# Two FFN layers: the first product by seven products of halves, and each FFN in two parts

## The chip, the cores and the metric

The kernel runs on one core of a Trainium2 chip, in one launch. The metric is the device time of one execution in microseconds (us). Five engines work side by side, each through its own list of instructions: PE multiplies matrices (PEld loads their stationary operand), DVE, ACT and POOL work on elements, SP issues the transfers from main memory. An instruction waits until what it reads is written and the buffer that it writes is free; what stands behind it on that engine waits with it.

## What is computed

The reference is a decoder trunk of two layers on x of 512 tokens by 1024 channels. Each layer has a mixer and a gated feed-forward network (FFN), and a layer norm behind each. The change is in the FFN alone:

```
def swiglu(x, w_in, w_out):
    h = x @ w_in                       # 1024 x 5632: gate columns, then up columns
    return (jax.nn.silu(h[..., :D_FF]) * h[..., D_FF:]) @ w_out
...
        x = layer_norm(ALPHA * x + mix, ln_mix_g[layer], ln_mix_b[layer])
        x = layer_norm(ALPHA * x + swiglu(x, ffn_w_in[layer], ffn_w_out[layer]),
                       ln_ffn_g[layer], ln_ffn_b[layer])
```

D_FF is 2816, and all is float32.

## The kernel before

Every float32 product is made of three products of rounded parts: `split` (L82 to L85) writes a rounded copy hi of its source (ACT, L84) and the rest lo = source − hi (DVE, or POOL for some, L85), and `mm3` (L87 to L90) issues the matmuls hi·hi, hi·lo and lo·hi into one PSUM bank. The transposed x stands in `xh` and `xl`: 1024 channels in 8 blocks of 128 (`KD`), 512 tokens beside each other. The plain x is kept in `xs` (the tiles x0 to x3 of 128 tokens, which the residual uses).

`ffn(l)` (L293) runs for each layer l. **First product:** for each of the 22 blocks n of 128 hidden columns, `load_cols` (L103) brings the gate block and the up block (512 KB each, into the pool `raw` of 3 buffers) and splits them into `wt` (8 buffers); `project` (L148) issues 2 × 8 × 3 = 48 matmuls of 512 tokens for the two; then ACT makes silu of the gate (L316), DVE multiplies by the up half (L318), and the result h is split into the tiles `hh` and `hl` that the second product reads. At block n = 6 (`XN`) `late_affine` (L192 to L202) is called: the norm ahead left x in `xs` without its scale and bias, and 16 element-wise operations of 128x512 on DVE put them in, in time for the residual; two transfers bring the vectors. **Second product:** `out_proj` (L286) takes 11 pairs kp of row blocks of w_out. A first pass makes output columns 0 to 511 for all four token tiles in four banks (two `fl`, two `sc`), a second pass columns 512 to 1023 (banks `py`, `cv`, `fl`, and at the very end `fl` and `sc`); of that pass 5 pairs are kept resident so that token tiles end one after the other. `residual` (L174 to L177) adds a finished bank to ALPHA times x, and `norm` (L204) follows.

PSUM has two banks `fl`, two `sc`, and one each of `py` and `cv` for all this, and two for transposes. A scheduler puts every engine's instructions in order when the program is built: it follows the order in which the code issues them, moves instructions ahead where it finds an engine idle in its own model, and honours the offset that `late_affine` gives its operations (a lower priority). On PE that holds in both FFNs; a fixed order for PE (`manual_schedule`) is used in the odd mixer alone. A buffer of a pool is handed on when the last reader of what it held is done: this makes the first instruction that writes the new tile wait for that reader.

Of the kernel before, what the change touches and what calls it, by code (L numbers as in the profile page):

```python
# [40 lines left out]
FIRST = 2  # L41
DFIRST = 2
DG = 1
XA = 2
XN = 6
# [13 lines left out]
def trunk(ctx, tc, x, ev_w_in, ev_conv_w, ev_pool_w, ev_pool_scale, ev_w_out, od_w_in,  # L59
# [109 lines left out]
    def load_gb(gb, g, b):  # L169
        nc.sync.dma_start(gb[:, 0, :], g.partition_broadcast(P))  # L170
        nc.sync.dma_start(gb[:, 1, :], b.partition_broadcast(P))
        return gb

    def residual(t, cols, acc, st):  # L174
        xc = xs[t][:, cols]
        nc.vector.scalar_tensor_tensor(xc, xc, ALPHA, acc, op0=ALU.mult, op1=ALU.add)
        nc.vector.bn_stats(st, xc)  # L177
# [26 lines left out]
    def norm(t, st, gb, ln):  # L204
# [11 lines left out]
        for a, b in PIECES:  # L216
            xc, g, b_ = xs[t][:, a:b], gb[:, 0, a:b], gb[:, 1, a:b]
# [12 lines left out]
    class OutProj:  # L230
# [3 lines left out]
        def __init__(self, w, order, lhs, resident, resident_pool=lambda kp: None, eng=None):  # L234
            self.w, self.order, self.lhs, self.resident = w, order, lhs, resident
            self.resident_pool, self.eng = resident_pool, eng
# [27 lines left out]
        def second(self, gb, ln):  # L264
            KP, order = len(self.order), self.order
            for t in range(NT):
                residual(t, slice(0, 512), self.accs[t][0][0], self.sts[t][:, 0, :])
                self.accs[t] = None
# [4 lines left out]
            for i in range(streamed):  # L273
                ws = self.load(order[i], 512)
                for t in range(NT):
                    self.step(t, i, ws)
            ws = [self.load(kp, 512, self.resident_pool(kp)) for kp in order[streamed:]]
            for t in range(NT):
                for part in range(len(self.accs[t])):
# [3 lines left out]
                    residual(t, slice(512 + cols.start, 512 + cols.stop), acc, self.sts[t][:, 1 + part, :])  # L283
# [8 lines left out]

    def ffn(l):  # L293
        w_in, w_out = ffn_w_in[l], ffn_w_out[l]
        with tc.tile_pool(name=f"ffn{l}", bufs=1) as hp:
            pairs = []
            gb = hp.tile([P, 2, D], F32, tag="gb", name="gb") if l else None
            for n in range(NF):
                if n == XN:
                    late_affine(ln_mix_g[l], ln_mix_b[l], nc.vector)  # L300
                if n == 4 and l:
                    load_gb(gb, ln_ffn_g[l], ln_ffn_b[l])
# [17 lines left out]
            out_proj(gb, 1 + 2 * l, w_out, list(range(NF // 2)), lambda k: [y[:, k % 2, :] for y in pairs[k // 2]],  # L320
# [537 lines left out]
```

## Time and profile before

| | us |
|---|---|
| median of 3 runs | 1117.99 (1117.77 to 1118.32) |
| the profiled execution, by the clock of the runs | 1118.16 |
| its span, first to last instruction | 1116.4 |
| FFN 0 in the trace: first product / second product | 159.7 to 394 / 394 to 516 |
| FFN 1: first product / second product | 746 to 988 / 988 to 1109 |

A profile is of one execution. The page lists busy time by engine, the chain of work that ended last, and groups of like instructions by line, with the mean duration of one and the idle time ahead; other views show one engine's instructions in order of time, or sums over a stretch. A granted clock of 1.00 is PE at full speed.

### The profile page before, as it was taken

The page shows a single profiled execution, that of the slowest core. Times are in us where ns is not written, and L with a number is a line of the kernel's source. Part 1 is how long each engine was busy: PE and PEld are TensorE (multiplying, and loading weights), DVE is VectorE, ACT ScalarE, POOL GpSimd, SP SyncE. Part 2 cuts the span into 40 slices and gives each one's busy share as a digit, 9 for nine tenths or more (in the row PEclk, how much of TensorE's full clock was granted, in tenths as well). Part 3 has the DMA queues.
Part 4 walks back from the last instruction along what each step waited for, and adds up shares of the span by engine and source line. Part 5 has one row for each costly group of instructions (what it writes and reads, how often), then busy time and mean ns, then how long its engine had stood idle before and what let it go on. Part 6 is the DMA issues. An engine that isn't in the chain of part 4 may idle for free.

```text
span 1116.4 us, 13508 instructions
## 1 busy us (share of the span) xinstructions
PE 1079.8 (97%) x5371; PEld 910.6 (82%) x5371; DVE 547.4 (49%) x821; ACT 395.5 (35%) x613; POOL 176.1 (16%) x160
## 2 busy tenths in 40 slices
PE   7999999999999999999999958999999999999997
PEld 7888898888888888889878746889888888888886
DVE  4845364633333322436689978564553333332426
ACT  4333134222233221223566838634232222222210
POOL 2000300000000000012797942520000000000003
PEclk9999999999999999999999979999999999999999
DMA  6423403343333222440332221333343333332312
GB/s 202 125 88 116 144 1 114 114 116 101 102 97 94 95 95 95 135 130 2 87 104 75 88 85 58 95 95 95 95 132 95 95 95 100 104 98 95 109 42 76
DMA packets 150332, 108.30 MB, mean 97 GB/s; under 512 B 5256, under 2 KB 131768, under 8 KB 150270
## 3 DMA queue, kind: packets, MB, share of 16 engines
q1 hardware_dynamic: 149648, 107.11, 31.9%
q8 instruction: 42, 0.69, 0.2%
q10 hardware_dynamic: 622, 0.34, 0.1%
q14 instruction: 20, 0.16, 0.1%
HBM read 103.17 MB, written 2.10 MB: 94 GB/s over the span
## 4 chain that ended last, share of the span: by engine, by line
PE 85%; DVE 7%; ACT 3%; POOL 3%; issue 1%; DMA 1%; SPq 0%; POOLq 0%; ACTq 0%
PE fl L88 11%; PE fl L89 11%; PE fl L90 11%; PE sc L89 9%; PE sc L90 9%; PE sc L88 9%; PE py L88 4%; PE py L89 4%; PE py L90 4%; PE cv L89 4%; PE cv L90 4%; PE cv L88 4%; DVE cv L466 2%; POOL convs L460 1%; DVE yc L85 1%
## 5 line engine op out<-in xcount | busy, mean ns | idle before, releaser
L84 ACT ACTIVATE w<-raw 128x1024 fp32r<-128x1024 f32 x176 | 185.9, 1060 | 538.1 <-PE sc L89 180.7
L85 DVE TENSOR_TENSOR w<-raw,w 128x1024 fp32r<-128x1024 f32 x148 | 180.7, 1224 | 287.5 <-ACT w L84 287.5
L85 POOL TENSOR_TENSOR w<-raw,w 128x1024 fp32r<-128x1024 f32 x28 | 67.4, 2415 | 450.6 <-ACT w L84 427.5
L89 PE MATMUL sc<-xl,w 128*128 128x512 f32 (+1 forms) x360 | 129.9, 361 | 0.0
L90 PE MATMUL sc<-xh,w 128*128 128x512 f32 (+1 forms) x360 | 129.6, 361 | 0.0
L88 PE MATMUL sc<-xh,w 128*128 128x512 f32 (+1 forms) x360 | 129.4, 362 | 0.0
L88 PE MATMUL fl<-xh,w 128*128 128x512 f32 (+1 forms) x352 | 128.6, 366 | 0.0
L89 PE MATMUL fl<-xl,w 128*128 128x512 f32 (+1 forms) x352 | 128.4, 365 | 0.0
L90 PE MATMUL fl<-xh,w 128*128 128x512 f32 (+1 forms) x352 | 128.3, 365 | 0.0
L166 POOL TENSOR_TENSOR rs<-rs,neghalf 128x1 f32<-128x1 f32 x20 | 14.4, 722 | 417.9 <-DVE rs L165 417.9
L89 PEld LDWEIGHTS sc<-xl,w 128*128 128x128 f32 x360 | 68.0, 189 | 10.3
L90 PEld LDWEIGHTS sc<-xh,w 128*128 128x128 f32 x360 | 68.0, 189 | 10.2
L88 PEld LDWEIGHTS sc<-xh,w 128*128 128x128 f32 x360 | 67.6, 189 | 10.4
L89 PEld LDWEIGHTS fl<-xl,w 128*128 128x128 f32 x352 | 66.5, 189 | 10.6
L88 PEld LDWEIGHTS fl<-xh,w 128*128 128x128 f32 x352 | 66.4, 189 | 10.6
L90 PEld LDWEIGHTS fl<-xh,w 128*128 128x128 f32 x352 | 66.3, 189 | 10.6
L89 PE MATMUL fl<-w,hh 128*128 128x512 f32 (+1 forms) x176 | 66.3, 377 | 0.0
L88 PE MATMUL fl<-w,hh 128*128 128x512 f32 (+1 forms) x176 | 66.1, 376 | 0.0
L90 PE MATMUL fl<-w,hl 128*128 128x512 f32 (+1 forms) x176 | 66.1, 376 | 0.0
L466 DVE SCALAR_TENSOR_TENSOR cv<-hp,par,cv 128x512 f32<-128x512 f32 x84 | 62.9, 749 | 5.2 <-ACT cv L454 3.9
L89 PE MATMUL py<-xl,w 128*128 128x512 f32 (+1 forms) x160 | 58.9, 368 | 0.0
L88 PE MATMUL py<-xh,w 128*128 128x512 f32 (+1 forms) x160 | 58.9, 368 | 0.0
(360 smaller groups left out, 2066.9 us busy)
## 6 DMA issues: line engine op xcount, KB each, us to landing
raw<-in_ffn_w_in SPq DMA_DIRECT2D x88, 512.0 KB
raw<-in_ffn_w_out SPq DMA_DIRECT2D x44, 512.0 KB
raw<-in_od_w_in SPq DMA_DIRECT2D x20, 512.0 KB
raw<-in_ev_w_in SPq DMA_DIRECT2D x16, 512.0 KB
raw<-in_ev_w_out SPq DMA_DIRECT2D x8, 512.0 KB
raw<-in_od_w_out SPq DMA_DIRECT2D x8, 512.0 KB
x<-in_x SPq DMA_DIRECT2D x4, 512.0 KB
qk<-qk SPq DMA_DIRECT2D x16, 128.0 KB
```

Of the source, the lines that this page charges most:

```text
L84: nc.scalar.activation(hi, src, AF.Copy)
L85: (eng or nc.vector).tensor_tensor(lo, src, f32(hi), op=ALU.subtract)
L88: nc.tensor.matmul(acc, lh, rh, start=start, stop=False)
L89: nc.tensor.matmul(acc, lh, rl, start=False, stop=False)
L90: nc.tensor.matmul(acc, ll, rh, start=False, stop=stop)
L166: nc.gpsimd.tensor_tensor(rs[:, 1:2], rs[:, 0:1], neghalf, op=ALU.pow)
L460: G.tensor_tensor(acc, acc, prod[:, i % 2, :], op=ALU.add)
L466: V.scalar_tensor_tensor(acc if i == KCONV - 1 else part, hp[:, i:i + S], tap(i), part, op0=ALU.mult, op1=ALU.add)
```

## The change

Blocks n = 0 to 3 (`PLAIN`) stay as they were. Blocks 4 to 21 go two at a time, a *group* for two blocks, and a class `Strassen` makes both halves (gate, up) of both blocks for all tokens in seven products in place of eight. The weights of a group are four quarters q11, q12 (gate columns, channels 0 to 511 and 512 to 1023) and q21, q22 (up columns), 128x1024 each; x is cut into four quarters by channels and tokens. `moving()` makes three further combinations of the x quarters once for each FFN and splits them (tiles T), and writes one more over a quarter of `xh` and `xl`. For each group four sums of weight quarters are made (POOL one, DVE three), and seven tiles are split: the quarters q11 (product P1), q12 (P2), q22 (P4), and the sums for P6, P5, P7 and P3. The split pairs lie in a ring `sw` of six tiles, that is three pairs. A product is 24 matmuls of 256 tokens. PE's order is fixed by hand: P1, P4 of the group before, P2, P3 of the group before, P6, P5, P7, and so on with P1 of the next group; the splits are issued in the order P1, P2, P6, P5, P7, P4, P3. Partial sums are read out of PSUM between the products (ACT `c1`, `u2`, `u3`; DVE L405, L417, L427), then silu, the multiplication (two `scalar_tensor_tensor`) and the split of h for two blocks at once.

Each FFN now runs in two parts: blocks 0 to 11 (`PART` = 12; four groups), then the second product over their six row pairs, added to ALPHA times x; then blocks 12 to 21 (five groups), and the second product over the other five row pairs, added to that (`alpha=1.0`), with the norm. `late_affine` is called behind the groups of part 1. The scale and bias of the last norm are loaded behind part 2's groups.

```diff
+PLAIN = 4
+PART = 12
+SHIFT = 16
-XN = 6
...
-def residual(t, cols, acc, st):
+def residual(t, cols, acc, st, alpha=ALPHA):
     xc = xs[t][:, cols]
-    nc.vector.scalar_tensor_tensor(xc, xc, ALPHA, acc, op0=ALU.mult, op1=ALU.add)
-    nc.vector.bn_stats(st, xc)
+    if alpha == 1.0:
+        nc.vector.tensor_tensor(xc, xc, acc, op=ALU.add)
+    else:
+        nc.vector.scalar_tensor_tensor(xc, xc, alpha, acc, op0=ALU.mult, op1=ALU.add)
+    if st is not None:
+        nc.vector.bn_stats(st, xc)
...
+        if ln is None:
+            for t in range(NT):
+                residual(t, slice(512, D), self.accs[t][0][0], None, self.alpha)
+            return
...
+class Strassen:
+    def __init__(self, hp):
+        self.hp, self.z = hp, itertools.cycle(("py", "cv"))
+    def block(self, kh, th):
+        ks, ts = slice(4 * kh, 4 * kh + 4), slice(256 * th, 256 * th + 256)
+        return xh[:, ks, ts], xl[:, ks, ts]
+    def moving(self):
+        V, G = nc.vector, nc.gpsimd
+        B = {(i, j): self.block(i, j) for i in range(2) for j in range(2)}
+        new = lambda: rawp.tile([P, 4, 256], F32, tag="raw", name="comb")
+        def less(eng, out, a, b):
+            t = wtp.tile([P, 4, 256], F32, tag="wt", name="combl")
+            eng.tensor_tensor(out, f32(a[0]), f32(b[0]), op=ALU.subtract)
+            eng.tensor_tensor(t, f32(a[1]), f32(b[1]), op=ALU.subtract)
+            eng.tensor_tensor(out, out, t, op=ALU.add)
+        def minus(out, a, b):
+            V.scalar_tensor_tensor(out, a, -1.0, f32(b[0]), op0=ALU.mult, op1=ALU.subtract)
+            V.tensor_tensor(out, out, f32(b[1]), op=ALU.subtract)
+        tile2 = lambda: [self.hp.tile([P, 4, 256], F32R, tag="T", name="T", bufs=6) for _ in range(2)]
+        t3, T3 = new(), tile2()
+        less(G, t3, B[1, 1], B[0, 1])
+        t1 = new()
+        less(V, t1, B[0, 0], B[0, 1])
+        t2, T2 = new(), tile2()
+        minus(t2, t1, B[1, 1])
+        split(*T2, t2)
+        split(*T3, t3)
+        split(*B[0, 1], t1)
+        t4, T4 = new(), tile2()
+        minus(t4, t2, B[1, 0])
+        split(*T4, t4)
+        self.B = dict(P1=B[0, 0], P2=B[1, 0], P3=B[1, 1], P4=T4, P5=B[0, 1], P6=T2, P7=T3)
+    def split(self, raw):
+        pair = [self.hp.tile([P, 4 * 256], F32R, tag="sw", name="sw", bufs=6).rearrange(
+            "p (k c) -> p k c", c=256) for _ in range(2)]
+        split(*pair, raw)
+        return pair
+    def stationary(self, w, n):
+        raw = {}
+        for key, row, c0 in (("11", 0, n * P), ("12", 512, n * P), ("21", 0, DFF + n * P),
+                             ("22", 512, DFF + n * P)):
+            raw[key] = wtp.tile([P, 4, 256], F32, tag="wt", name="q" + key)
+            nc.sync.dma_start(raw[key], w[row:row + 512, c0:c0 + 256].rearrange("(k p) c -> p k c", p=P))
+        add = lambda a, b, eng=nc.vector: self.added(a, b, eng)
+        A = {}
+        A["P1"] = self.split(raw["11"])
+        A["P2"] = self.split(raw["12"])
+        s3 = add(raw["11"], raw["21"], nc.gpsimd)
+        s1 = add(raw["21"], raw["22"])
+        s2 = add(s1, raw["11"])
+        A["P6"] = self.split(s2)
+        A["P5"] = self.split(s1)
+        A["P7"] = self.split(s3)
+        A["P4"] = self.split(raw["22"])
+        A["P3"] = self.split(add(s2, raw["12"]))
+        return A
+    def added(self, a, b, eng):
+        out = rawp.tile([P, 4, 256], F32, tag="raw", name="sum")
+        eng.tensor_tensor(out, a, b, op=ALU.add)
+        return out
+    def product(self, g, name, bank, start=False, stop=False):
+        (ah, al), (bh, bl) = g["A"][name], self.B[name]
+        for i in range(2):
+            acc, cols = bank[:, i * 256:(i + 1) * 256], slice(i * P, (i + 1) * P)
+            for k in range(4):
+                for m, (l, r) in enumerate(((ah, bh), (ah, bl), (al, bh))):
+                    nc.tensor.matmul(acc, l[:, k, cols], r[:, k, :], start=start and i == k == m == 0,
+                                     stop=stop and i == 1 and k == 3 and m == 2, skip_group_check=True)
+    def begin(self, w, n, out):
+        return dict(A=self.stationary(w, n), out=out)
+    halves = staticmethod(lambda t, j: t.rearrange("p (i s) -> p i s", i=2)[:, :, 256 * j:256 * (j + 1)])
+    whole = staticmethod(lambda t: t.rearrange("p (i s) -> p i s", i=2))
+    def first(self, g, name):
+        V, S_ = nc.vector, nc.scalar
+        if name == "P1":
+            g["x"], g["c1"] = psum("fl"), wk.tile([P, 512], F32, tag="h", name="c1")
+            self.product(g, "P1", g["x"], start=True)
+            S_.activation(g["c1"], g["x"], AF.Copy)
+        elif name == "P2":
+            z = psum(next(self.z))
+            g["h"] = self.hp.tile([P, 2 * S], F32, tag="g", name="g", bufs=2)
+            self.product(g, "P2", z, start=True, stop=True)
+            V.tensor_tensor(self.halves(g["h"], 0), self.whole(z), self.whole(g["c1"]), op=ALU.add)
+        elif name == "P6":
+            g["u2"] = wk.tile([P, 512], F32, tag="sg", name="u2")
+            self.product(g, "P6", g["x"])
+            S_.activation(g["u2"], g["x"], AF.Copy)
+        elif name == "P5":
+            g["y"] = psum("sc")
+            self.product(g, "P5", g["y"], start=True)
+        else:
+            g["u3"] = wk.tile([P, 512], F32, tag="h", name="u3")
+            self.product(g, "P7", g["x"])
+            S_.activation(g["u3"], g["x"], AF.Copy)
+            V.tensor_tensor(g["u3"], g["u3"], g["y"], op=ALU.add)
+    def last(self, g, name):
+        V, S_ = nc.vector, nc.scalar
+        if name == "P4":
+            self.product(g, "P4", g["x"], stop=True)
+        else:
+            self.product(g, "P3", g["y"], stop=True)
+            h = g["h"]
+            V.tensor_tensor(self.halves(h, 1), self.whole(g["y"]), self.whole(g["u2"]), op=ALU.add)
+            S_.activation(h, h, AF.Silu)
+            for j, up in enumerate((g["x"], g["u3"])):
+                V.scalar_tensor_tensor(self.halves(h, j), self.whole(up), -1.0, self.halves(h, j),
+                                       op0=ALU.mult, op1=ALU.mult)
+            hh, hl = g["out"]
+            split(hh, hl, h.rearrange("p (i s) -> p i s", i=2))
 def ffn(l):
     w_in, w_out = ffn_w_in[l], ffn_w_out[l]
     with tc.tile_pool(name=f"ffn{l}", bufs=1) as hp:
         pairs = []
-        gb = hp.tile([P, 2, D], F32, tag="gb", name="gb") if l else None
-        for n in range(NF):
-            if n == XN:
-                late_affine(ln_mix_g[l], ln_mix_b[l], nc.vector)
-            if n == 4 and l:
-                load_gb(gb, ln_ffn_g[l], ln_ffn_b[l])
+
+        def new_pair():
+            pairs.append([hp.tile([P, 2, S], F32R, tag="h", name=nm, bufs=PART) for nm in ("hh", "hl")])
+            return pairs[-1]
+
+        lhs = lambda k: [y[:, k % 2, :] for y in pairs[k // 2]]
+        for n in range(PLAIN):
...
-                tag = "hA" if n < 10 else "hB"
-                pairs.append([hp.tile([P, 2, S], F32R, tag=tag, name=nm, bufs=10 if n < 10 else 12)
-                              for nm in ("hh", "hl")])
+                new_pair()
...
-        out_proj(gb, 1 + 2 * l, w_out, list(range(NF // 2)), lambda k: [y[:, k % 2, :] for y in pairs[k // 2]],
-                 5, lambda kp: [dict(pool_=hp, tag="hA", bufs=10)] * 2)
+        st = Strassen(hp)
+        st.moving()
+        hp.tile([P, SHIFT], F32, tag="shift", name="shift")
+        def groups(ns):
+            before = None
+            with tc.manual_schedule(engines={mybir.EngineType.PE}):
+                for n in ns:
+                    g = st.begin(w_in, n, new_pair())
+                    for name, late in (("P1", "P4"), ("P2", "P3"), ("P6", None), ("P5", None), ("P7", None)):
+                        st.first(g, name)
+                        if before and late:
+                            st.last(before, late)
+                    before = g
+                for late in ("P4", "P3"):
+                    st.last(before, late)
+        groups(range(PLAIN, PART, 2))
+        late_affine(ln_mix_g[l], ln_mix_b[l], nc.vector)
+        o = OutProj(w_out, list(range(PART // 2)), lhs, 0)
+        for i in range(PART // 2):
+            o.first(i)
+        o.second(None, None)
+        groups(range(PART, NF, 2))
+        gb = None
+        if l:
+            g_, b_ = (hp.tile([P, 4 * 256], F32, tag="sw", name="gb", bufs=6) for _ in range(2))
+            nc.sync.dma_start(g_, ln_ffn_g[l].partition_broadcast(P))
+            nc.sync.dma_start(b_, ln_ffn_b[l].partition_broadcast(P))
+            gb = g_, b_
+        spare = iter([dict(pool_=hp, tag="T", bufs=6)] * 6 + [dict(pool_=hp, tag="sw", bufs=6)] * 2)
+        out_proj(gb, 1 + 2 * l, w_out, list(range(PART // 2, NF // 2)), lhs, 4,
+                 lambda kp: [next(spare), next(spare)], alpha=1.0)
```

The rows below are the instructions of an engine in the order of the built program (line, operation, output tile <- inputs, size; the number of a tile tells one allocation from the next). The first two fences are DVE and ACT in the changed kernel where group 16 follows group 14 in part 2 of FFN 0. L87 is the lo half of a split and L86 its hi half, L376 a sum of weight quarters, L405, L417, L427 and L430 work on products that are done; `sw` is the ring of split pairs. On DVE, from the lo half for P7 of group 14 to the lo half for P1 of group 16:

```order
L87 TENSOR_TENSOR sw_3467<-sum_3452,sw_3466 128x1024
L430 SCALAR_TENSOR_TENSOR g_3300<-fl_3248,g_3300 128x2x256
L430 SCALAR_TENSOR_TENSOR g_3300<-u3_3407,g_3300 128x2x256
L376 TENSOR_TENSOR sum_3686<-q21_3672,q22_3674 128x1024
L87 TENSOR_TENSOR sw_3471<-q22_3442,sw_3470 128x1024
L87 TENSOR_TENSOR hl_3203<-g_3300,hh_3202 128x1024
L87 TENSOR_TENSOR sw_3477<-sum_3474,sw_3476 128x1024
L376 TENSOR_TENSOR sum_3688<-sum_3686,q11_3668 128x1024
L87 TENSOR_TENSOR sw_3677<-q11_3668,sw_3676 128x1024
```

On ACT at the same place, with the counts of other engines that each instruction waits for; sw_3676 is the hi half for that P1, and its wait on PE is for the last matmul that reads sw_3466, the hi half for P7 of group 14:

```order
L86 ACTIVATE sw_3470<-q22_3442 128x1024 [waits DMAHW2_49,PE_49,Activation_49]
L409 ACTIVATE u2_3588<-fl_3480 128x512 [waits PE_49]
L86 ACTIVATE hh_3202<-g_3300 128x1024 [waits DVE_49,Activation_49]
L86 ACTIVATE sw_3476<-sum_3474 128x1024 [waits PE_49]
L86 ACTIVATE sw_3676<-q11_3668 128x1024 [waits DMAHW3_49,PE_49]
L416 ACTIVATE u3_3639<-fl_3480 128x512 [waits PE_49]
```

Before, the same engine, DVE, in the first product of FFN 0 (L85 the lo half of a split, L318 gate times up) has two weight tiles, one gate times up and one h in turn:

```order
L85 TENSOR_TENSOR w_1597<-raw_1594,w_1596 128x1024
L318 TENSOR_TENSOR h_1518<-sc_1315,sg_1516 128x512
L85 TENSOR_TENSOR w_1603<-raw_1600,w_1602 128x1024
L85 TENSOR_TENSOR hl_1509<-h_1518,hh_1508 128x512
L85 TENSOR_TENSOR w_1665<-raw_1662,w_1664 128x1024
```

So seven tiles are now split for two blocks in a ring of three pairs, where it was four in a pool of four pairs.

The second place is DVE where the affine operations stand. In the changed kernel it is the step from group 8 to group 10 in part 1 of FFN 0 (L203 are the affine operations on x0 to x3, sw_2114 the lo half for P1 of group 10, sw_2118 that for its P2):

```order
L87 TENSOR_TENSOR sw_2114<-q11_2105,sw_2113 128x1024
L203 TENSOR_TENSOR x0_74<-x0_74,gb_2622 128x512 x2
L417 TENSOR_TENSOR u3_2076<-u3_2076,sc_2051 128x512
L203 TENSOR_TENSOR x1_75<-x1_75,gb_2622 128x512 x2
L203 TENSOR_TENSOR x2_76<-x2_76,gb_2622 128x512 x2
L203 TENSOR_TENSOR x3_77<-x3_77,gb_2622 128x512 x2
L203 TENSOR_TENSOR x0_74<-x0_74,gb_2623 128x512 x2
L203 TENSOR_TENSOR x1_75<-x1_75,gb_2623 128x512 x2
L203 TENSOR_TENSOR x2_76<-x2_76,gb_2623 128x512 x2
L203 TENSOR_TENSOR x3_77<-x3_77,gb_2623 128x512
L87 TENSOR_TENSOR sw_2118<-q12_2107,sw_2117 128x1024
L203 TENSOR_TENSOR x3_77<-x3_77,gb_2623 128x512
```

Before, they stood on DVE (L202) behind the h of block 5:

```order
L85 TENSOR_TENSOR hl<-h,hh 128x512
L202 TENSOR_TENSOR x_74<-x_74,gb 128x512 x2
L202 TENSOR_TENSOR x_75<-x_75,gb 128x512 x2
L202 TENSOR_TENSOR x_76<-x_76,gb 128x512 x2
L202 TENSOR_TENSOR x_77<-x_77,gb 128x512 x2
L202 TENSOR_TENSOR x_74<-x_74,gb 128x512 x2
L202 TENSOR_TENSOR x_75<-x_75,gb 128x512 x2
L318 TENSOR_TENSOR h<-sc,sg 128x512
L202 TENSOR_TENSOR x_76<-x_76,gb 128x512
L85 TENSOR_TENSOR w<-raw,w 128x1024
```

They moved from there to a place between the lo halves of two products that PE takes with one other product between them.

The third place is the start of part 1 of FFN 0 in the changed kernel, on DVE, behind the last gate times up of the plain blocks but one (L459, h_1588). L329 and L330 make the combination for P4, T_1662 and T_1685 are the lo halves of `moving()` for P7 and P4, xl_79 the quarter written over, sum_1715 the sum for P6 and sw_1718 its lo half:

```order
L87 TENSOR_TENSOR sw_1708<-q12_1697,sw_1707 128x1024
L87 TENSOR_TENSOR T_1662<-comb_1660,T_1661 128x1024
L329 SCALAR_TENSOR_TENSOR comb_1683<-comb_1672,xh_78 128x1024
L330 TENSOR_TENSOR comb_1683<-comb_1683,xl_79 128x1024
L87 TENSOR_TENSOR xl_79<-comb_1667,xh_78 128x4x256
L87 TENSOR_TENSOR T_1685<-comb_1683,T_1684 128x1024
L376 TENSOR_TENSOR sum_1713<-q21_1699,q22_1701 128x1024
L459 TENSOR_TENSOR h_1656<-fl_1593,sg_1654 128x512
L376 TENSOR_TENSOR sum_1715<-sum_1713,q11_1695 128x1024
L87 TENSOR_TENSOR hl_1585<-h_1656,hh_1584 128x512
L87 TENSOR_TENSOR sw_1718<-sum_1715,sw_1717 128x1024
```

What moved: five operations of `moving()` now stand ahead of the first two sums of group 4.

More of the change, by code (lines that the diff above doesn't have):

```diff
@@ L216, in norm @@
         for a, b in PIECES:
-            xc, g, b_ = xs[t][:, a:b], gb[:, 0, a:b], gb[:, 1, a:b]
+            xc, g, b_ = xs[t][:, a:b], gb[0][:, a:b], gb[1][:, a:b]
             if b == D:
```

14 lines of the change are left out of this document (6 added, 8 removed).

## The prediction

> **What bounds the kernel now.** I read the page's busy times and its chain of waits first, then the sums over two stretches of the FFN's first product.
>
> ```profile
> PE 1079.8 (97%) x5371; PEld 910.6 (82%) x5371; DVE 547.4 (49%) x821; ACT 395.5 (35%) x613; POOL 176.1 (16%) x160
> PE 85%; DVE 7%; ACT 3%; POOL 3%; issue 1%; DMA 1%; SPq 0%; POOLq 0%; ACTq 0%
> ```
>
> The first row is busy time by engine, the second the chain that ended last, by engine. PE is the bound: only work taken from PE, or idle time given to it, moves the end. In a stretch of 100 us (columns: length, PE, PEld, DVE, ACT, POOL busy with counts, granted clock, DMA share, GB/s):
>
> ```profile
> 200.00:300.00 100.00, 100.00 (x443) 82.81 (x442) 44.28 (x54) 28.44 (x37) 0.00 (x0) 1.00 0.36 106
> 300.00:400.00 100.00, 100.00 (x443) 82.81 (x442) 33.59 (x36) 28.44 (x36) 0.00 (x0) 1.00 0.33 100
> ```
>
> PE is never idle there, at full clock. DVE has more than half of its time free, and 443 matmuls in 100 us are 225.7 ns for one of 512 tokens. Nothing that the change does to ACT, DVE or the transfers can save time here; it saves only what it takes from PE.
>
> **What it takes from PE.** The price of a matmul of 256 tokens stands in the first projection of the even mixer, where PE runs such matmuls without a gap:
>
> ```profile
> 16.53 0.28 PE L88 MATMUL fl<-xh,w 128*128 128x256 f32 x1
> ...
> 17.25 0.28 PE L88 MATMUL fl<-xh,w 128*128 128x256 f32 x1
> ```
>
> These two are six matmuls apart, 0.72 / 6 = 120 ns each. A group was 2 × 48 × 225.7 ns = 21.67 us of PE; it becomes 7 × 24 = 168 matmuls × 120 ns = 20.16 us. The saving is 1.51 us in a group. There are 9 groups in each FFN, 18 in all: **−27.2 us**. The eighth part in arithmetic (12.5%) shrinks to 7%, as 256 tokens cost more than half of 512. The second product keeps its matmuls, and a group brings the same 2 MB as its two blocks did, over engines that are busy to a third (0.33 to 0.36 above), so I cost the transfers at nothing.
>
> **What a group asks of the other engines.** In one group of 20 us there are seven splits of 128x1024, four sums of 128x1024, three reads of partial sums by DVE, three by ACT, silu, two multiplications, and the split of h:
>
> ```profile
> L84 ACT ACTIVATE w<-raw 128x1024 fp32r<-128x1024 f32 x176 | 185.9, 1060 | 538.1 <-PE sc L89 180.7
> L85 DVE TENSOR_TENSOR w<-raw,w 128x1024 fp32r<-128x1024 f32 x148 | 180.7, 1224 | 287.5 <-ACT w L84 287.5
> L85 POOL TENSOR_TENSOR w<-raw,w 128x1024 fp32r<-128x1024 f32 x28 | 67.4, 2415 | 450.6 <-ACT w L84 427.5
> ...
> L318 DVE TENSOR_TENSOR h<-sc,sg 128x512 f32<-128x512 f32 x15 | 10.4, 691 | 41.5 <-PE sc L90 40.8 <-ACT sg L316 0.7
> L422 DVE SCALAR_TENSOR_TENSOR y<-cv,par,y 128x512 f32<-128x512 f32 x8 | 6.0, 748 | 0.1
> ```
>
> The fields before the last bar are total busy us and mean ns of one. DVE: 7 + 3 + 1 = 11 × 1.22, three × 0.69, two × about 0.72 = 17 us of 20. ACT: 8 × 1.06 + 1.06 + 3 × 0.6 = 11 us. POOL: one sum, 2.4 us. All fits in sum, but DVE goes from about a third busy to 85%, and its order decides.
>
> **The wait at each step from group to group.** In the order of the changed program, the hi half for the next P1 may be written only when P7 of this group has read its own, since when P7 runs, the three pairs of the ring hold P7, P4 and P3 (both still to come). In the old kernel ACT's idle time before such a split was for PE too (180.7 us of it in the first row above), but with a pool of four pairs PE had the next pair ready and did not wait for it. Now PE does: P1's first matmul needs hi, the third needs lo. The least wait is hi 1.06 + lo 1.22 + 0.1 of hand-over − two matmuls of 0.12 = 2.1 us. DVE can make it longer, as eight operations stand ahead of that lo. I put P3 of the group before, ending, at 0 on PE: P6, P5, P7 take 3 × 24 × 0.120 = 8.64, and the third matmul of P1 would be due at 8.88. On DVE the lo for P5 comes after P2's pair is free: hi 0 − 2.88 + 1.06 = −1.8, lo −0.6; then the sum s2 + q12 until 0.65. POOL's sum for the next group waits for that one's buffer, and so runs from 0.65 to 3.05, just when the lo for P7 is due. What that does to DVE stands in the odd mixer:
>
> ```profile
> 638.85 12.04 DVE L85 TENSOR_TENSOR yc<-yatt,yc 128x512 fp32r<-128x512 f32 x1
> 650.81 0.15 DVE L661 RECIPROCAL sm<-sm 128x1 f32<-128x1 f32 x1
> ```
> ```profile
> 639.36 1.31 POOL L85 TENSOR_TENSOR wql<-raw,wqh 128x512 fp32r<-128x512 f32 x1
> ...
> 649.04 1.30 POOL L460 TENSOR_TENSOR convs<-convs,prod 128x512 f32<-128x512 f32 x1
> ```
> ```profile
> 18.04 2.48 DVE L85 TENSOR_TENSOR pwl<-pwr,pwh 128x512 fp32r<-128x512 f32 x1 [0.66 <-ACT pwh L84]
> ```
> ```profile
> 17.56 2.40 POOL L85 TENSOR_TENSOR w<-raw,w 128x1024 fp32r<-128x1024 f32 x1 [3.21 <-ACT w L84]
> ```
>
> A DVE operation of 0.69 us with both inputs in SBUF took 12.04 us, until POOL's row of additions was over, and in the second pair 2.48 us beside one POOL operation. So the lo for P7 runs from 3.05 to 4.27. Behind it stand two multiplications (0.69, 0.75), then six of 1.22 (next sum, lo for P4, lo of h, lo for P3, next sum, lo for P1): 8.76, less about 0.5 as neighbours overlap. That gives 12.5 for the lo of P1, and a wait of 12.5 + 0.2 − 8.9 = 3.8 us, with small hand-overs 4.0, 1.1 of it before P1's first matmul and 2.8 before its third. There are 14 such steps (3 + 4 in each FFN); in the first of each part 2 the buffers are fresh, POOL runs early, and I take 2.2. **12 × 4.0 + 2 × 2.2 = +52.4 us**, with bounds of 14 × 2.2 = 31 (POOL blocks nothing) and 14 × 4.3 = 60 (no overlap of neighbours).
>
> The Trainium skill (SBUF — State Buffer, "Who interferes with whom") says that a DVE instruction with two SBUF inputs contends with a GpSimd instruction that reads SBUF, and that whoever comes second is fully blocked; it speaks against the POOL sum of this change, and the 12.04 us above agree with it. By that rule the steps cost 52 us, without it 31.
>
> **The start of part 1.** Between the last plain block and P6 stand, on DVE, the lo for P7's combination 1.22, the two steps of P4's combination 1.27 + 1.22, the overwritten quarter 1.22 (it may only be written when the last plain matmul is done), the lo for P4's combination 1.22, a sum 1.22, h 0.69, POOL's 2.4 in between, and the sum for P6 1.22; then ACT's hi 1.06. That is 12.7 from the end of the plain blocks; P1 and P2, split ahead, cover 5.76. P6 is late by 7.0, and P6's lo adds 0.5: **2 × 7.5 = +15**, with bounds of 2 and 9 each (2 if the combinations are done before the plain blocks end; 9 if POOL's chain for P7 also holds DVE up).
>
> **The late affine.**
>
> ```profile
> L202 DVE TENSOR_TENSOR x<-x,gb 128x512 f32<-128x512 f32 x32 | 19.8, 682 | 12.0 <-DMA gb<-in_ln_mix_g 12.0
> ```
> ```profile
> 216.94 1.88 DVE L202 TENSOR_TENSOR x<-x,gb 128x512 f32<-128x512 f32 x3
> 218.75 1.22 DVE L85 TENSOR_TENSOR w<-raw,w 128x1024 fp32r<-128x1024 f32 x1
> ```
>
> The same 16 operations as before, mixed then among splits in a stretch where PE waited for nothing (200 to 300 above), as DVE had 56% to spare. Now 15 of them stand between the lo for P1 and the lo for P2 in one step from group to group: 15 × 0.68 = 10.2, about 1 for their transfers, the third partial sum 0.69 and the lo 1.22 make 13.1; of that PE covers the rest of P1 and P4, 22 × 0.12 + 24 × 0.12 + two matmuls of P2 = 5.76. PE stands for about 7. In the second FFN I take 5.6, as the transfers are ready: **+12.6**, bounds 0 and 8 each (0 if the vectors come early enough for some of them to run in DVE's gaps).
>
> **Between the parts.** The second product of part 1 frees its banks through four more residuals in each pass and FFN:
>
> ```profile
> L176 DVE SCALAR_TENSOR_TENSOR x<-x,sc 128x512 f32<-128x512 f32 x8 | 5.5, 683 | 0.5 <-PE sc L90 0.5
> ```
>
> The 8 additional ones in each FFN (5.5 us of DVE) stand beside matmuls, but those that free a bank stand behind sums and splits of part 2's first group, and PE waits for the bank: I take 5 us in each FFN, near the middle of 0 and 7: **+10**. If all of DVE's work there were hidden it would be 0; 7 is six operations of 1.22 ahead of a residual.
>
> **The clock.** Where PE stands long, it comes back at half speed (columns: length, PE busy, clock, DMA share, GB/s):
>
> ```profile
> 642.00:644.00 2.00, 1.28 (x6) 1.00 0.00 0
> 644.00:646.00 2.00, 0.00 (x0) 1.00 0.00 0
> 646.00:648.00 2.00, 0.00 (x0) 0.65 0.46 151
> ...
> 654.00:656.00 2.00, 1.96 (x7) 0.50 0.00 0
> ...
> 660.00:662.00 2.00, 2.00 (x12) 0.94 0.29 66
> ```
>
> PE stopped at 643.3; the clock fell at 646.6 (0.65 is the mean of 0.6 us at 1.00 and 1.4 at 0.50), 3.3 us later. PE went on at 654.0 and had its full clock again at 660.2: 6.2 us at half speed, which cost 3.1. The gaps at P6 and at the affine operations, two in each FFN, are longer than 3.3 us: 4 × 3.1 = 12, of which I take **+8**, bounds 0 and 12.
>
> **The sum.** −27.2 + 52.4 + 15 + 12.6 + 10 + 8 = +70.8. The profiled execution took 1118.16 (span 1116.4 and 1.8 around it; the median of the runs is 1117.99, 0.02% less). 1118.2 + 70.8 = **1189 us**, 6.3% slower.
>
> **The rivals.**
>
> *POOL does not hold DVE up here.* Beside this POOL operation two of DVE ran at their usual length, one with an input in PSUM, one with a single input:
>
> ```profile
> 123.94 2.40 POOL L85 TENSOR_TENSOR w<-raw,w 128x1024 fp32r<-128x1024 f32 x1 [1.91 <-ACT w L84]
> ```
> ```profile
> 124.39 0.69 DVE L176 SCALAR_TENSOR_TENSOR x<-x,fl 128x512 f32<-128x512 f32 x1 [8.80 <-PE fl L90]
> 125.11 0.69 DVE L177 BATCH_NORM_STATS2 st<-x 128x6 f32<-128x512 f32 x1
> ```
>
> Against it stand the 12.04 us, with the same kinds of operands as the splits. Then 14 × 2.2 = 31 in place of 52.4, P6 late by 5.1 in place of 7.5, half of the clock's loss: −27.2 + 31 + 10 + 12.6 + 10 + 4 = +40, **1159**. Chance 0.08.
>
> *The clock falls at most steps.* If two matmuls in the middle of a wait of 4 us do not count as work, a fall of 3.1 at nine of the twelve long steps adds 28: **1217**. For it: the wait is longer than 3.3 us in all. Against it: neither of its pieces, 1.1 and 2.8, is. Chance 0.09. The Trainium skill (TensorE: Matmul & The Clock Gate, Part 1) puts the fall after an idle window of about 3.4 us, in windows that run freely; the 3.3 us above agree with it, and by it the two pieces would not do. No row here shows a gap with two matmuls in it.
>
> *The faster side: P1's pair is free before P7 is done.* The place is the step from group to group. Were P1's pair one that P5 or an earlier product has read, hi and lo (2.3 us) would fit into P7's 2.88 us, the 52.4 would go, and DVE, no longer late at the steps, would run ahead at the affine operations and the parts as well. With the rest at 10 in all: −27.2 + 10, **1101**. It decides from 1.9 us at each step (27.2 / 14): below that, with the rest small, the change gains. The order of ACT speaks against it: that hi waits for PE, and PE's count is P7's last reading. Chance 0.03.
>
> **How the numbers follow.** The forecast has 0.80. All its terms at their lower bounds but the steps' (48 with POOL's hold) give −27.2 + 48 + 4 = +25; all at the upper give −27.2 + 60 + 18 + 16 + 14 + 12 = +93. That all fall on one side is unlikely; the range goes from 1150, which takes in the first rival, to 1217, the second. Faster by over 0.2% (about what a measurement of this kernel can tell from no change) 0.03, within it 0.01, slower 0.96.
>
> **What would show it.** In the changed kernel's profile: PE at 120 ns a matmul in the products, and PE idle for about 1.1 and 2.8 us at P1 of each group, the first ended by ACT's hi (L86), the second by DVE's lo (L87); a DVE lo of 2.4 us or more beside POOL's sum (L376); idle PE of some 7 us before P6 of the groups 4, and some 7 before P2 of the groups 10, with a clock of 0.5 behind. PE's busy time should fall by about 27 us apart from stretches at half clock. I am wrong if P1's lo is on time: then the steps cost 31 or nothing, and DVE's queue was not late.

## The result, and the profile after

| | before | after |
|---|---|---|
| median, us | 1118.15 (1117.77 to 1118.90, 4 runs) | 1180.12 (1179.31 to 1182.87, 4 runs) |
| ratio | | 1.0558, 95% interval 1.0539 to 1.0576 |
| span of the profiled execution, mean clock | 1116.4, 0.991 | 1177.6, 0.957 |

The change makes the kernel 5.6% slower, 62 us. The forecast was 1189. The page's first part, busy time by engine, in the changed kernel:

```profile
PE 1077.2 (91%) x6631; PEld 966.2 (82%) x6631; DVE 780.2 (66%) x1003; ACT 486.2 (41%) x693; POOL 239.7 (20%) x184
```

PE went from 97% of the span to 91%; it is busy 2.6 us less, though it does much less, since part of that is at half clock. Sums of what PE waited for (line, awaited instruction: us in total, times, longest):

```profile
PE fl L385 <- DVE sw L87: 32.7, 16, 3.0
PE fl L385 <- ACT sw L86: 26.6, 16, 6.2
PE py L864 <- DVE tl L87: 11.1, 2, 10.7
...
PE py L385 <- DVE sw L87: 4.0, 2, 2.4
...
PE fl L385 <- DVE x L176: 2.4, 2, 1.2
```

L385 is a matmul of the products, so four of these rows are new, 65.7 us together; the third is the odd mixer's, as before (11.2). ACT's `sw` is the hi half of a split, DVE's the lo half. The step from group 16 to group 18 by PE, ACT, DVE and POOL in order of time (start, length, instruction, idle ahead and what ended it). It is the step whose order was shown with the change; the text there, and some expectations below, number the groups wrongly: those rows are of groups 16 and 18, and the affine operations stand in the step from group 6 to 8, ahead of P2 of group 8.

```profile
430.92 2.88 PE L385 MATMUL fl<-T,sw 128*128 128x256 f32 x24
434.83 0.39 PE L385 MATMUL fl<-xh,sw 128*128 128x256 f32 x1 [1.03 <-ACT sw L86]
435.06 0.28 PE L385 MATMUL fl<-xl,sw 128*128 128x256 f32 x1
438.33 0.80 PE L385 MATMUL fl<-xh,sw 128*128 128x256 f32 x2 [2.99 <-DVE sw L87]
```
```profile
433.72 1.06 ACT L86 ACTIVATE sw<-q 128x1024 fp32r<-128x1024 f32 x1 [0.28 <-PE fl L385]
```
```profile
426.95 3.19 DVE L87 TENSOR_TENSOR sw<-sum,sw 128x1024 fp32r<-128x1024 f32 x1
430.06 0.68 DVE L430 SCALAR_TENSOR_TENSOR g<-fl,g 128x512 f32<-128x512 f32 x1
...
435.91 1.23 DVE L376 TENSOR_TENSOR sum<-sum,q 128x1024 f32<-128x1024 f32 x1
437.06 1.22 DVE L87 TENSOR_TENSOR sw<-q,sw 128x1024 fp32r<-128x1024 f32 x1
```
```profile
426.65 2.40 POOL L376 TENSOR_TENSOR sum<-q,q 128x1024 f32<-128x1024 f32 x1 [23.76 <-issue]
```

P7 is the row of 24 matmuls. ACT starts P1's hi when P7 is done; PE waits 1.03 for it, makes two matmuls, and waits 2.99 for the lo, which stands last in DVE's row without a gap from 426.95. That row begins with the lo for P7, 3.19 us long in place of 1.22: POOL's sum is over at 429.05, and this lo 1.09 later, about its own length. This is called POOL's hold below. Each of these was in the working ahead of the run.

The other gaps of PE in FFN 0 are at P6 of group 4, at P2 of group 8 behind the affine operations, and at the bank for part 2's first product:

```profile
209.96 0.80 PE L385 MATMUL fl<-T,sw 128*128 128x256 f32 x2 [6.21 <-ACT sw L86]
211.22 5.06 PE L385 MATMUL fl<-T,sw 128*128 128x256 f32 x22 [0.46 <-DVE sw L87]
...
258.67 0.50 PE L385 MATMUL py<-xh,sw 128*128 128x256 f32 x2 [2.43 <-DVE sw L87]
...
370.31 0.35 PE L385 MATMUL fl<-xh,sw 128*128 128x256 f32 x1 [1.23 <-DVE x L176]
```

The second row runs 22 matmuls in 5.06 us: half clock. The clock about the step above (stretch: length, PE busy, granted clock, DMA share, GB/s):

```profile
435.00:437.00 2.00, 0.34 (x2) 1.00 0.26 91
437.00:439.00 2.00, 0.67 (x3) 0.77 0.00 0
439.00:441.00 2.00, 2.00 (x11) 0.50 0.00 0
441.00:443.00 2.00, 2.00 (x17) 0.87 0.00 0
```

It falls at a step too, although neither piece of the wait is longer than 3.0 us. In stretches of 0.5 us through both FFNs it falls 14 times: at both P6 and at 12 of the 14 steps. Before, it did not fall in either FFN.

And the price of a matmul. These two are 24 apart:

```profile
229.46 0.28 PE L385 MATMUL cv<-xh,sw 128*128 128x256 f32 x1
...
232.18 0.28 PE L385 MATMUL sc<-xh,sw 128*128 128x256 f32 x1
```

2.72 / 24 = 113.3 ns, not 120. In other stretches (376 to 382, 471 to 485) it is 117.8; the mean over all products at full clock is about 115.

### The profile page after: what moved, and what is told of

It reads as the page before. It is cut to its first block, busy times and chain, and to the rows that moved or that the text cites. A ratio compares the mean times of both kernels' runs of the same rounds, so it can differ in the third digit from the quotient of the medians.

```text
span 1177.6 us, 16398 instructions
## 1 busy us (share of the span) xinstructions
PE 1077.2 (91%) x6631; PEld 966.2 (82%) x6631; DVE 780.2 (66%) x1003; ACT 486.2 (41%) x693; POOL 239.7 (20%) x184
## 5 line engine op out<-in xcount | busy, mean ns | idle before, releaser
L86 ACT ACTIVATE w<-raw 128x1024 fp32r<-128x1024 f32 x104 | 109.6, 1060 | 202.6 <-PE sc L91 57.4
L385 PE MATMUL fl<-T,sw 128*128 128x256 f32 x1296 | 166.1, 286 | 13.0 <-ACT sw L86 12.1
L385 PEld LDWEIGHTS fl<-T,sw 128*128 128x128 f32 x1296 | 161.4, 197 | 14.3 <-ACT sw L86 12.5
L87 DVE TENSOR_TENSOR w<-raw,w 128x1024 fp32r<-128x1024 f32 x76 | 95.2, 1258 | 110.9 <-ACT w L86 110.9
L376 POOL TENSOR_TENSOR sum<-q,q 128x1024 f32<-128x1024 f32 x18 | 47.1, 2615 | 485.7 <-DVE sum L376 204.2
L87 DVE TENSOR_TENSOR sw<-sum,sw 128x1024 fp32r<-128x1024 f32 x72 | 110.9, 1543 | 34.6 <-ACT sw L86 34.6
L385 PE MATMUL fl<-xh,sw 128*128 128x256 f32 x288 | 79.3, 366 | 48.8 <-DVE sw L87 31.8
L86 ACT ACTIVATE sw<-q 128x1024 fp32r<-128x1024 f32 x54 | 57.4, 1063 | 157.1 <-PE fl L385 120.0
L87 DVE TENSOR_TENSOR sw<-q,sw 128x1024 fp32r<-128x1024 f32 x54 | 66.1, 1225 | 83.2 <-ACT sw L86 83.2
L86 ACT ACTIVATE sw<-sum 128x1024 fp32r<-128x1024 f32 x72 | 76.0, 1061 | 108.2 <-PE fl L385 31.0
L385 PEld LDWEIGHTS fl<-xh,sw 128*128 128x128 f32 x288 | 63.6, 264 | 55.4 <-DVE sw L87 34.6
L385 PE MATMUL sc<-xh,sw 128*128 128x256 f32 x576 | 105.5, 278 | 0.0
L87 POOL TENSOR_TENSOR w<-raw,w 128x1024 fp32r<-128x1024 f32 x28 | 67.4, 2414 | 186.0 <-ACT w L86 162.9
L385 PEld LDWEIGHTS sc<-xh,sw 128*128 128x128 f32 x576 | 90.2, 188 | 0.0
L385 PE MATMUL sc<-xl,sw 128*128 128x256 f32 x288 | 80.1, 278 | 0.0
L90 PE MATMUL sc<-xh,w 128*128 128x256 f32 (+1 forms) x168 | 54.9, 331 | 0.0
L92 PE MATMUL sc<-xh,w 128*128 128x256 f32 (+1 forms) x168 | 54.8, 328 | 0.0
```

The lines of the kernel that those rows point to most:

```text
L86: nc.scalar.activation(hi, src, AF.Copy)
L87: (eng or nc.vector).tensor_tensor(lo, src, f32(hi), op=ALU.subtract)
L90: nc.tensor.matmul(acc, lh, rh, start=start, stop=False)
L92: nc.tensor.matmul(acc, ll, rh, start=False, stop=stop)
L376: eng.tensor_tensor(out, a, b, op=ALU.add)
L385: nc.tensor.matmul(acc, l[:, k, cols], r[:, k, :], start=start and i == k == m == 0, stop=stop and i == 1 and k == 3 and m == 2, skip_grou ...
```

## The experiments

Each kernel is timed beside the kernel before the change on the same chip (1118.8, 1119.4 and 1118.8 in the three sessions). Theory A of the first three is the forecast's own: the ring makes PE wait at each step, and POOL's sum makes that wait longer.

### The pair for P1 split ahead of the pair for P3

```diff
             A["P1"] = self.split(raw["11"])
+            if before:
+                before["A"]["P3"] = self.split(self.s5)
             A["P2"] = self.split(raw["12"])
...
-            A["P3"] = self.split(add(s2, raw["12"]))
+            self.s5 = add(s2, raw["12"])
```

> Only the order in which splits are issued changes: the pair for P3 of the old group is split after the pair for P1 of the next one, so P1's pair no longer waits for P7. Theory A (the ring of pairs): the wait at P1 (1.2 + 3.1 us at ten of the 14 steps, 1.2 + 0.9 at four) falls under 1 us, most of the clock's falls at the steps go too, and the time falls by 35 to 65 us from 1180, to 1115 to 1145. Theory B (DVE is late whatever the ring does): only the 1.2 us before P1's first matmul goes, about 15 us, to 1165, and the wait for DVE's lo stays near 3 us.

1133.6 us (ratio 1.0130, 1.0113 to 1.0147): 46.5 less than the change, inside theory A. The step from group 14 to 16 on PE:

```profile
395.38 0.28 PE L387 MATMUL fl<-xh,sw 128*128 128x256 f32 x1
395.49 0.28 PE L387 MATMUL fl<-xl,sw 128*128 128x256 f32 x1
397.66 0.66 PE L387 MATMUL fl<-xh,sw 128*128 128x256 f32 x2 [1.90 <-DVE sw L87]
```

P1 no longer waits for its hi, and for its lo 1.9 us here, 1.4 to 1.9 at ten steps and nothing over 0.3 at four. So the wait is not under 1 us everywhere, as A had it: DVE stays late by its own queue and POOL's hold (the lo for P7 takes 3.19 here as well). The clock falls eight times in place of 14. The gap behind the affine operations rose to 4.9 and 4.7 us.

The edit does two things at once: P1 gets a pair that is free earlier, and its lo stands elsewhere on DVE. In the same step, the lo for P1, the lo for P3 and the next group's second sum:

```profile
396.39 1.21 DVE L87 TENSOR_TENSOR sw<-q,sw 128x1024 fp32r<-128x1024 f32 x1
397.53 1.21 DVE L87 TENSOR_TENSOR sw<-sum,sw 128x1024 fp32r<-128x1024 f32 x1
...
399.26 1.21 DVE L378 TENSOR_TENSOR sum<-sum,q 128x1024 f32<-128x1024 f32 x1
```

The last two stood ahead of P1's lo before. That lo now ends 2.1 us after P7 in place of 4.5, about what the two operations take. So at the ten long steps DVE's row set the length of the wait. At the four short ones, where DVE was on time, the whole 1.8 us went, and that was the ring. More pairs in the ring, with the old order, were not tried.

### POOL's sum left out

```diff
-            s3 = add(raw["11"], raw["21"], nc.gpsimd)
...
-            A["P7"] = self.split(s3)
+            A["P7"] = self.split(raw["21"])
```

> Leaves out the sum q11 + q21 that POOL makes in each group; P7 splits q21 itself. Nothing else runs on POOL in the groups. Theory A (POOL's sum holds DVE's lo for P7 up): the second piece of the wait falls from 2.9 to about 0.8 us at the ten long steps, 21 us, and with shorter falls of the clock 20 to 30 us go: 1150 to 1160. Theory B (DVE's queue is long by itself): 1177 to 1183, the second piece stays at 2.9.

1154.0 us (1.0331, 1.0291 to 1.0371), 26 less: theory A. The second piece of the wait is 0.76 at 12 steps and 1.5 and 2.0 at two, those behind the affine operations. The gap at P2 of group 8 grew to 3.9 in FFN 0 and 1.9 in FFN 1.

### The sum on DVE

```diff
-            s3 = add(raw["11"], raw["21"], nc.gpsimd)
+            s3 = add(raw["11"], raw["21"])
```

> The same sum on DVE (1.2 us) in place of POOL (2.4 us). Theory A: DVE is held up 2.4 us by POOL and now works 1.2 us instead, so the second piece falls from 2.9 to about 1.7 us at the ten long steps, 10 to 15 us in all: 1165 to 1170. Theory B (no hold): DVE's queue gets 1.2 us longer at each step: 1190 to 1197.

1148.6 us (1.0269, 1.0254 to 1.0285), 31.5 less, more than expected. The lo halves of sums on DVE, as a group (busy us, mean ns, idle ahead), in the changed kernel:

```profile
L87 DVE TENSOR_TENSOR sw<-sum,sw 128x1024 fp32r<-128x1024 f32 x72 | 110.9, 1543 | 34.6 <-ACT sw L86 34.6
```

and with the sum on DVE, where also a step of PE:

```profile
L87 DVE TENSOR_TENSOR sw<-sum,sw 128x1024 fp32r<-128x1024 f32 x72 | 87.6, 1221 | 35.8 <-ACT sw L86 35.8
```
```profile
401.74 0.38 PE L385 MATMUL fl<-xh,sw 128*128 128x256 f32 x1 [1.03 <-ACT sw L86]
403.00 0.50 PE L385 MATMUL fl<-xh,sw 128*128 128x256 f32 x2 [0.76 <-DVE sw L87]
```

The hold goes (72 × 0.32 = 23 us of DVE), and DVE's row now ends before ACT's hi, although the sum's 1.2 us were added to it. Its end in the same step, the lo for P3, the lo for P1 and the next group's second sum:

```profile
400.30 1.22 DVE L87 TENSOR_TENSOR sw<-sum,sw 128x1024 fp32r<-128x1024 f32 x1
401.72 1.23 DVE L87 TENSOR_TENSOR sw<-q,sw 128x1024 fp32r<-128x1024 f32 x1 [0.21 <-ACT sw L86]
...
403.46 1.22 DVE L376 TENSOR_TENSOR sum<-sum,q 128x1024 f32<-128x1024 f32 x1
```

The scheduler has put that second sum behind P1's lo, which makes up for the one added. (With POOL's sum left out, the next group's first sum had moved ahead of the row.) So neither kernel takes away the hold alone. By the rows of the changed kernel the hold is 3.19 − 1.22 = 1.97 us; without it 1.0 of the 2.99 us would be left, an estimate. What is left at most steps, 1.03 + 0.76 to 0.90, is about the least wait of the ring: hi, then lo; behind the affine operations the second piece is still 3.1 and 3.2. Theory B falls. A was right in its cause and too small in size; the gaps at P6 (4.8 us each) and at P2 of group 8 (0.3) became shorter as well.

### Matmuls in the waits that nobody reads

```diff
+                self.fill(9)
                 self.product(g, "P1", g["x"], start=True)
...
+                        if name == "P1" and i == k == 0 and m == 1:
+                            self.fill(22)
```

> At each P1, 9 matmuls of 256 that nobody reads are issued before it (1.0 us) and 22 more behind its second matmul (2.5 us), so that PE is busy in both pieces of the wait. Theory C (the clock falls at the steps because PE is idle there for about 4 us): the clock stays at 1.00 at the steps, 12 falls of about 2.3 us each go, the four short steps and the two starts of a part without a wait lose some 2 to 3 us each (15 in all): 1163 to 1173. Theory D (the falls come from something else, the waits cost only their own length): the falls stay, and the time rises by 10 to 20 us, 1190 to 1200.

1180.6 us (1.0551, 1.0535 to 1.0567), the same as the change. The clock about a step of part 2, whose P1 starts at 438.77 (stretch: length, PE busy, clock, DMA share, GB/s):

```profile
437.00:439.00 2.00, 2.00 (x18) 1.00 0.61 165
439.00:441.00 2.00, 2.00 (x18) 1.00 0.29 97
441.00:443.00 2.00, 1.64 (x14) 1.00 0.00 0
```

Theory C is right about the clock: all falls at the steps are gone, four remain at P6 and behind the affine operations (where PE now waits 4.5 and 4.2 us). Its time is wrong: 31 matmuls in each of 18 groups are about 69 us on PE, the waits that they replaced 50, and the rest of the waits stays, so what the clock gave was spent again. The falls come from PE's idle time at the steps; a filler of this size does not pay.

### The FFNs in two parts, with plain blocks

`groups(...)` is replaced by the plain loop over the same blocks, and the affine step called at block 6.

> The FFNs in two parts, all blocks as before the change (no products of halves, no ring, late affine at block 6): the other part of the change alone. In the trace of the changed kernel the hand-over between the parts cost two gaps of 1.2 us on PE for a bank, 2.4 us in both FFNs, and the second product took 2 us longer in each. Theory A (the parts cost little): 1118 to 1124. Theory B (my forecast's 5 us in each FFN): 1126 to 1130.

1118.2 us against 1119.4, ratio 0.9988 (0.9972 to 1.0005): no difference that can be told, theory A. PE's waits hold no line of the FFNs.

### The affine step later

```diff
-            late_affine(ln_mix_g[l], ln_mix_b[l], nc.vector)
+            late_affine(ln_mix_g[l], ln_mix_b[l], nc.vector,
+                        lambda: hp.tile([P, D], F32, tag="sw", name="gb", bufs=6))
```

> The changed kernel, only the two vectors of the late affine step are loaded into tiles of the ring, which come free when part 1's products are done; so its 16 operations run beside the second product. Theory A (they delay the lo for P2 of group 10, 2.4 and 1.5 us, and keep DVE late behind it): the two gaps go, 5 to 12 us with what hangs on them: 1168 to 1175. Theory B (DVE would be as late there for the ring and the POOL sum, or the operations now delay the residuals): 1177 to 1183.

1173.0 us (1.0480, 1.0453 to 1.0507), 7 less: theory A. Both gaps at P2 of group 8 are gone, the steps stay as they were, and the clock still falls 14 times.

### Three edits, then all

First the order of the splits, the sum on DVE and the affine step together.

> Three edits together: the order of the splits (1133.6 alone), the sum on DVE, the affine step later. With the ring's wait gone, what is left in the trace of that order is 4.5 and 4.2 us at the affine steps, each with a fall of the clock (2 to 3 us), 3.5 us at each P6 and small waits of 0.4 for DVE. If the terms add: 1133.6 - 8.7 - 5 - 3 = 1117, range 1110 to 1122. If DVE's load decides (18 us of work in a group of 19): the waits come back elsewhere, 1125 to 1140.

1104.1 us (0.9867, 0.9841 to 0.9894): 1.3% under the kernel before the change, and a larger gain than the sum of the terms. PE waits 0.6 to 1.1 us for P1's lo at ten steps, the clock falls at P6 alone. Then, on top, the matmuls on hi first in P1 and P6, and the combination for P7 on DVE:

```diff
+                        if name in ("P1", "P6") and m == 2:
+                            continue
...
+            if name in ("P1", "P6"):
...
+                        nc.tensor.matmul(acc, al[:, k, cols], bh[:, k, :], start=False,
...
-            less(G, t3, B[1, 1], B[0, 1])
...
+            t3, T3 = new(), tile2()
+            less(V, t3, B[1, 1], B[0, 1])
```

> As the one before, and P1 and P6 issue their 16 matmuls that read hi first and the 8 that read lo last, and the combination for P7 is made on DVE behind that for P6. If a wait for lo is covered by matmuls on hi, and P6 of the first group comes 2 to 3 us earlier in each FFN with a shorter fall of the clock: 8 to 15 us under the one before, 1098 to 1110, under the kernel before the change (1118). If DVE's load decides: within 3 us of the one before.

**1085.6 us**, ratio 0.9694 (0.9667 to 0.9720): 3.1% faster than the kernel before the change, 94 us faster than the change, below what was expected. What PE waited for in the products, and a stretch of part 1 (length; PE, PEld, DVE, ACT, POOL busy; clock, DMA share, GB/s):

```profile
PE fl L390 <- ACT sw L87: 6.5, 2, 3.5
```
```profile
220.00:280.00 60.00, 60.00 (x500) 59.47 (x499) 50.83 (x53) 34.15 (x38) 0.00 (x0) 1.00 0.20 62
```

Only P6 is left, 3.0 and 3.5 us, beside 0.2 and 0.3 us for the bank of part 2's first product. The two edits on top were not tried one by one. PE has no gap in 60 us, while DVE is busy 85% of them: its load fits, as the forecast had it, if nothing in its order stands in the way.

### Without the unused tile

```diff
-            hp.tile([P, SHIFT], F32, tag="shift", name="shift")
```

In the changed kernel, and in the fastest one:

> The changed kernel without the unused tile of 16 words (SHIFT), which moves the address of the ring sw behind it and has no other use. In the changed kernel a matmul of 256 tokens took 113 ns in some stretches and 118 in others. Theory A (the address plays no part): 1177 to 1183, the same two spacings. Theory B (the pad keeps reads of the ring apart from others): the products run at 118 to 120 ns throughout, 3024 matmuls by some 4 ns: 1190 to 1200.

> The fastest kernel so far (1085.6) without the same tile. Theory A: 1083 to 1088. Theory B: 1095 to 1105.

1183.1 us (1.0567, 1.0532 to 1.0602), no clear difference, and 1099.4 us (0.9823, 0.9792 to 0.9855), 13.8 more. In both the price of a matmul changed. Two matmuls that are 24 apart, in the changed kernel without the tile:

```profile
230.34 0.28 PE L385 MATMUL cv<-xh,sw 128*128 128x256 f32 x1
...
233.22 0.28 PE L385 MATMUL sc<-xh,sw 128*128 128x256 f32 x1
```

2.88 / 24 = 120 ns, nearly throughout. So B holds for the matmul, though not its reason, which nothing here shows; its time came true only where PE waits for next to nothing. In the changed kernel the products became longer and the waits shorter (2.36 for the lo in place of 3.0 at the later steps of part 2), as DVE had more time: what the tile gains there, the waits eat.

## Why the forecast was right, step by step

The time came out 9 us under the forecast, in the range; but the terms did not all hold, and their errors go against each other.

| term | forecast | in the trace |
|---|---|---|
| arithmetic | −27.2 | about −42 |
| 14 steps | +52.4 | 46.3 |
| P6 of group 4 | +15 | 13.0 |
| late affine | +12.6 | 4.0 |
| hand-over | +10 | 2.4 |
| clock | +8 | about 30 |

The waits are PE's idle times as shown; each of 36 pieces cost about 0.16 more, since a matmul is drawn 0.28 long and the next may start after 0.12: 6 us. The sum is then 60 of the 61 us between the two spans.

- **The steps** held in place, cause and size. Ten were 3.5 to 4.0 us, as worked out; four, and not only two, were short (1.8): the first of part 1 too. The new order of the splits shows the issue order as the cause: the ring alone makes the 1.8 us of the short steps, and at the long ones it is DVE's row, with the lo for P1 at its end. POOL's hold in that row is read from the rows (3.19 in place of 1.22), and the two kernels without POOL's sum agree, though the order on DVE changed in them too.
- **P6** held; DVE's row is without a gap from the lo for P7's combination (197.73) to the sum for P6 (until 208.8), and POOL's sum is in it: the quarter written over took 3.43 us in place of 1.22.
- **The arithmetic** failed as a size: 120 ns was read from another place in the program. There it is true, and here as well without the unused tile, which I had passed over; with it a matmul took 113 to 118. That is 18 × 168 × 5 ns = 15 us.
- **The clock** failed as a size, and in its step: I gave it to the four longest gaps, as neither piece of a step's wait reached 3.3 us. It fell at 12 of 14 steps. That was the second rival, and its mechanism happened; its 1217 did not come, as the other terms were smaller. The 3.3 us were no threshold: at P6 of group 4 PE stopped at 203.75, and the clock fell at 205.99, 2.2 us later. PE was busy 66 us at half clock, where a matmul took 213 ns in place of 115, so 1 − 115/213 = 46% of it is lost: 30 us, an estimate. The filled waits show that the idle time is the cause.
- **The affine step** was too large by 8.6. On DVE and PE in FFN 0:

```profile
249.57 7.91 DVE L203 TENSOR_TENSOR x<-x,gb 128x512 f32<-128x512 f32 x13
257.40 1.22 DVE L87 TENSOR_TENSOR sw<-q,sw 128x1024 fp32r<-128x1024 f32 x1
```
```profile
247.67 0.79 PE L385 MATMUL fl<-xh,sw 128*128 128x256 f32 x2 [2.91 <-DVE sw L87]
...
255.96 0.28 PE L385 MATMUL py<-xl,sw 128*128 128x256 f32 x1
```

  From P1's third matmul to the lo for P2 it was 11.0 us, not 13.1 (the vectors were there, and neighbours on DVE overlap), and PE covered 8.6 of them, not 5.76, as its clock had fallen. What the one term lost, the clock's term holds. Moved away alone, the affine operations gave 7 us with what hung on them.
- **The hand-over** was guessed, near the middle of its bounds, and was 1.2 us in each FFN. The two parts alone cost nothing.

So the sign was safe (the waits alone are more than the saving), while the closeness owes something to luck: 15 us more of saving, and 16 less at the affine step and the hand-over, stand against 22 more for the clock.

The faster side had named its place rightly, but not what it takes: P1's pair freed earlier gave 1133.6 by itself, not 1101, as DVE stayed late and the gaps at P6 and at the affine operations remained. With the four other edits the same products make the kernel 3.1% faster than before.

## What to carry to other kernels

A ring of buffers that is handed on in the order of issue can tie the first user of the next group to the last of this one; look for the instruction that is awaited and what stands ahead of it on its engine, and try the order of the splits (here it gave 46 us; more buffers were not tried). Work that fits in sum (DVE 85% busy) may still be late at every step, and a short wait of PE can cost the clock as well: 1.8 us of waiting, where the clock fell for 3.4 us behind it, cost by the 46% above about 1.6 us more. A saving in PE's arithmetic is only seen when the waits are gone, and so is the worth of a tuned detail such as the unused tile.

## What the runs showed of the hardware

- **The clock falls for waits in pieces.** In the changed kernel, at a step with 1.03 and 0.76 us idle, two matmuls between, the clock fell too (at 386.89), while at another with 1.08 and 0.76 (222.9) it did not. The Trainium skill (TensorE: Matmul & The Clock Gate, Part 1) speaks of an idle window of about 3.4 us that runs freely. By a rule of one idle stretch of that length these falls would not come; the trace has them. It has the window too: all falls in both FFNs lie whole numbers of 3.413 us apart (205.99 to 246.95 is 12 of them, 246.95 to 386.89 is 41). On that grid, the stretch that ended in the fall at 386.89, and the two that share the wait at 222.9 (stretch: length, PE busy, clock, DMA share, GB/s):

```profile
383.48:386.89 3.41, 1.70 (x13) 1.00 0.86 271
```
```profile
219.64:223.05 3.41, 2.33 (x20) 1.00 0.86 252
223.05:226.47 3.42, 2.66 (x22) 1.00 0.47 145
```

  Nearly all of the first wait, both pieces, lies in one stretch, where PE was busy 50% of the time; the second wait is cut in two by the border, with 68% and 78%. In the changed kernel each stretch at full clock with PE busy at most 50% ended in a fall, and none with 52% or more did. In the other traces the border lies near one half as well, less sharply (between 0.42 and 0.53). So the same wait costs the clock or not, by where it meets the grid. This is read from the traces; no run was made for it.
- **The price of a matmul changed with the place of the stationary tiles.** 113 to 118 ns with the ring 16 words further on, 120 without, for the same 256 tokens, in two kernels. What in the addresses does it, and what switches between 113.3 and 117.8 from one stretch to the next, stays open.
- **DVE held up by POOL.** A DVE subtraction of 1.22 us took 3.19 beside POOL's sum of 2.40 that had begun 0.3 us earlier, and 3.19 again with the new order of the splits; with the sum moved, the mean is 1.22. At the start of part 1 it went both ways: POOL's sum, begun 0.1 us behind a DVE subtraction (200.24, 1.22 us), took 3.39 us, and the DVE operation behind that subtraction 3.43.
